# Final norm of a decoder trunk: one VectorE step folded into the squares' sum, one output piece issued from ScalarE's queue

## The chip, the cores and the metric

The kernel runs on one core of one Trainium2 chip. The metric is device time in microseconds for one launch. Three runs of the kernel before took 1069.72, 1070.24 and 1070.36 us; the median is 1070.24 us. A profile is one further execution, recorded by the hardware profiler.

## The reference

One decoder layer on 256 tokens of width 2048, in float32: a norm, a combined input projection, eight heads of forgetting attention and eight of dilated attention, an output projection with a residual add, a norm, a squared-ReLU MLP of width 8192 with a residual add, and one last norm. Cut to what matters here:

```python
def rms_norm(x, g):
    y = x * lax.rsqrt(jnp.mean(x * x, axis=-1, keepdims=True) + NORM_EPS)   # NORM_EPS = 1e-6
    return y * g

h = rms_norm(x, norm1_g);  proj = h @ w_in            # 2048 -> 6152 columns
... attention ...
x = x + mixed @ w_out
h = rms_norm(x, norm2_g)
x = x + jnp.square(jax.nn.relu(h @ w_mlp_in)) @ w_mlp_out
return rms_norm(x, final_norm_g)
```

The MLP's two products are the bulk of the work: 2048 x 8192 and 8192 x 2048 weights, 256 tokens.

## The kernel before

**Matmuls.** Every float32 matrix product is made of three products in the fast float32r format: each operand is split into a high part (`hi`, a rounded copy made by ScalarE) and a rest (`lo`, a subtraction by VectorE), and hi·hi, hi·lo and lo·hi are summed in a PSUM bank. Weights come from HBM by DMA into `raw` tiles, are split into `whi` and `wlo`, and go to TensorE. The statement `matmul(acc, a, b)` keeps `a` in the array as the stationary operand (128 columns, brought there by a weight load of its own before each matmul) and streams `b` past it as the moving operand (256 or 512 columns). A row of the profile such as `bank<-whi,mix_hi` names the moving operand first and the stationary one second. Three lines issue nearly all matmuls: L521 (products whose result is wanted transposed: the up projection of the MLP, and queries and keys; the weights are stationary, `aT_hi`/`aT_lo` move), L505 (plain products: the weights move, the activations are stationary) and L585 (a scheme that saves one in eight block products in the values' projection and in the MLP's down projection; again the weights move).

**Places in SBUF.** Tiles come from pools that are laid out one behind the other in each partition: `lead_in`, `one`, `two`, `wraw`, `wsplit`, `wide`, `few`, and behind `few` the pool `mix` during attention, which is closed before the MLP and replaced by `late5` and `late`. Tile starts are set by hand: constants such as `HIGH, LOW, NEAR` (L43) and `MIX_HI, MIX_LO` (L44), in float32 elements, are offsets inside a larger tile, and small filler tiles stand in front of others (`mix_begin` L112, `late_begin` L1238, `late_hi` and `late_low` L1246 and L1248). Weight parts go to four slots of `wsplit` and, in the MLP, to a fifth one, `whi5`/`wlo5` in `late5`: each fifth split is put there (L249). `late` holds `mix_hi` and `mix_lo`, the activations that L585 uses as stationary operands beside `big_hi` and `big_lo` of `wide`. The pool `few` holds small per-token numbers; each of its tiles takes a slot of 32 bytes per partition or a multiple of it.

**Order.** The order of the work is written out by hand: a list of half weight tiles (`steps`), each with two slots, and side work such as draining a bank that is attached to a slot (`at`). Engines run their own lists in that order.

**The end.** The last weight chunk (`last_chunk`, L1099) is done token half by token half: first 128 tokens (t = 0), then the other 128 (t = 1) as two products of 256 columns. For each, `add_down` (L1059) adds the product to the residual `xs` and, for the last columns, sums their squares on VectorE (L1070, a multiply that also accumulates, followed by a read of the accumulator into `ssq3`). `sum_before` (L1075) has summed the squares of the earlier columns into `ssq3s`, with 2048·eps added. `finish` (L1080) then makes the mean `v` (L1085), takes its power of -0.5 on GpSimd (L1086), multiplies the last columns with the gain (`put_gain`), sharpens the root by one Newton step (L1088, L1089), makes the product `ru` for ScalarE on GpSimd (L1090), and scales the row in four pieces of 384, 512, 512 and 640 columns. Pieces 0, 2 and 3 are scaled by VectorE (L1096), piece 1 by ScalarE (L1094). All four are sent to HBM from SyncE's queue (L1097), in the order 0, 1, 2, 3.

Of the kernel before, what the change touches and what calls it, by code (L numbers as in the profile page):

```python
# [11 lines left out]
F32 = mybir.dt.float32  # L12
# [3 lines left out]
ALU = mybir.AluOpType  # L16
# [3 lines left out]
P = 128  # L20
D_MODEL = 2048
# [8 lines left out]
EPS = 1e-6  # L30
# [45 lines left out]
def kernel(  # L76
# [18 lines left out]
    nc = tc.nc  # L95
    x2d = x.rearrange("b (t p) d -> p (b t) d", p=P)
    o2d = out.rearrange("b (t p) d -> p (b t) d", p=P)
# [9 lines left out]
    few = ctx.enter_context(tc.tile_pool(name="few", bufs=1))  # L107
# [893 lines left out]
    ssq3 = few.tile([P, TB, 5], F32, name="ssq3")  # L1001
    ssq3s = few.tile([P, TB], F32, name="ssq3s")
    rstd3 = few.tile([P, TB], F32, name="rstd3")
# [9 lines left out]
    def drain_d(r, c, ci):  # L1013
        for t in range(TB):
            add_down(accs[ci][t], t, slice(c * CW, (c + 1) * CW), None)
        give_back(*accs.pop(ci))
# [36 lines left out]
    def square_and_gain(t, cs, n):  # L1053
        unused = two.tile([P, CW], F32, name="nat")
        nc.scalar.activation(unused[:, :cs.stop - cs.start], xs[:, t, cs], AF.Square, accum_out=ssq3[:, t, n:n + 1])
        if n > 2:
            put_gain(t, cs)

    def add_down(acc, t, cs, n):  # L1059

        nc.vector.scalar_tensor_tensor(
            xs[:, t, cs], acc[:, :cs.stop - cs.start], rstd2sq[:, t:t + 1], xs[:, t, cs], op0=ALU.mult, op1=ALU.add
        )
        if n is not None:
            if cs.stop < D_MODEL:
                square_and_gain(t, cs, n)
            else:
                unused = two.tile([P, CW], F32, name="nat")
                unused, xc, total = unused[:, :cs.stop - cs.start], xs[:, t, cs], ssq3[:, t, n:n + 1]
                nc.vector.tensor_tensor_reduce(unused, xc, xc, 1.0, 0.0, ALU.mult, ALU.add, total)  # L1070

    def put_gain(t, cs):
        nc.vector.tensor_tensor(xs[:, t, cs], xs[:, t, cs], late_tiles["gf"][:, cs], op=ALU.mult)

    def sum_before(t, n):  # L1075
        s = ssq3s[:, t:t + 1]
        nc.vector.tensor_reduce(s, ssq3[:, t, :n], axis=mybir.AxisListType.X, op=ALU.add)
        nc.vector.tensor_scalar(s, s, D_MODEL * EPS, None, op0=ALU.add)

    def finish(t, n, cs):  # L1080
        r, s = rstd3[:, t:t + 1], ssq3s[:, t:t + 1]
        v = few.tile([P, 1], F32, name="fi_v", bufs=2)
        u = few.tile([P, 1], F32, name="fi_u", bufs=2)
        ru = few.tile([P, 1], F32, name="fi_ru", bufs=2)
        nc.vector.tensor_scalar(v, ssq3[:, t, n:n + 1], s, 1.0 / D_MODEL, op0=ALU.add, op1=ALU.mult)  # L1085
        nc.gpsimd.tensor_tensor(r, v, half_t[:, :1], op=ALU.pow)  # L1086
        put_gain(t, cs)
        nc.vector.scalar_tensor_tensor(u, r, v, r, op0=ALU.mult, op1=ALU.mult)  # L1088
        nc.vector.tensor_scalar(u, u, -0.5, 1.5, op0=ALU.mult, op1=ALU.add)  # L1089
        nc.gpsimd.tensor_tensor(ru, r, u, op=ALU.mult)  # L1090
        for c, (a, b) in enumerate(((0, 384), (384, 896), (896, 1408), (1408, 2048))):
            xc = xs[:, t, a:b]
            if c == 1:
                nc.scalar.activation(xc, xc, AF.Copy, scale=ru)  # L1094
            else:
                nc.vector.tensor_scalar(xc, xc, r, u, op0=ALU.mult, op1=ALU.mult)  # L1096
            nc.sync.dma_start(o2d[:, t, a:b], xc)  # L1097

    def last_chunk(done):  # L1099

        ci = len(chunks) - 1
        what, key, _, _, _, _, kts = chunks[ci]
        i0 = len(steps) - kts // 2
        c0 = D_MODEL - CW
        half = CW // 2
        for t, a, b, n in ((0, 0, CW, 3), (1, 0, half, 3), (1, half, CW, 4)):
            acc = take_bank()
            for kt in range(kts):
                if t == 0 and kt % 2 == 0:
                    split(done + 1 + kt // 2)  # L1110
                    load_gf()
                for c in range(a, b, half):
                    product(acc[:, c - a:c - a + half], operands(what, key), kt, t, splits[i0 + kt // 2], kt % 2,
                            slice(c, c + half), kt == 0 and c == a, kt == kts - 1, True)
                if t == 0:
                    run_side(2 * i0 + kt)
            if b == CW:
                sum_before(t, n)
            add_down(acc, t, slice(c0 + a, c0 + b), n)
            if b == CW:  # L1120
                finish(t, n, slice(c0 + a, c0 + b))
# [6 lines left out]
    for ci, (what, key, *_rest) in enumerate(chunks[:-1]):  # L1128
# [12 lines left out]
        elif what in "qk":  # L1141
# [4 lines left out]
            if what == "k":  # L1146
                kind = groups[key][4]
                for h in range(4):
                    n = e + 5 + 5 * h
# [141 lines left out]
```

## Time and profile before

| | us |
|---|---|
| median of three runs | 1070.24 |
| the profiled execution | 1070.14 |
| its span, first to last instruction | 1068.4 |
| TensorE busy | 1057.8 |
| VectorE busy | 881.1 |
| ScalarE busy | 636.5 |
| GpSimd busy | 87.6 |
| mean granted TensorE clock | 0.997 of full |

The span is what the hardware profiler saw on the core; the profiled execution's own time is 1.7 us longer, with what lies around the span. Shares of busy time overlap, since the engines work side by side. A row of the timeline gives start, duration, engine, line and operation; when rows of TensorE follow each other without a gap, the distance of their starts is what one of them costs, and not the duration in the row, since matmuls overlap. A row of the chain gives start, length and number of the instructions in one piece of the chain that ended last.

### The profile page before, as it was taken

The page shows a single profiled execution, that of the slowest core. Times are in us where ns is not written, and L with a number is a line of the kernel's source. Part 1 is how long each engine was busy: PE and PEld are TensorE (multiplying, and loading weights), DVE is VectorE, ACT ScalarE, POOL GpSimd, SP SyncE. Part 2 cuts the span into 40 slices and gives each one's busy share as a digit, 9 for nine tenths or more (in the row PEclk, how much of TensorE's full clock was granted, in tenths as well). Part 3 has the DMA queues.
Part 4 walks back from the last instruction along what each step waited for, and adds up shares of the span by engine and source line. Part 5 has one row for each costly group of instructions (what it writes and reads, how often), then busy time and mean ns, then how long its engine had stood idle before and what let it go on. Part 6 is the DMA issues. An engine that isn't in the chain of part 4 may idle for free.

```text
span 1068.4 us, 21120 instructions
## 1 busy us (share of the span) xinstructions
PE 1057.8 (99%) x8720; PEld 1031.3 (97%) x8720; DVE 881.1 (82%) x1197; ACT 636.5 (60%) x887; POOL 87.6 (8%) x90
## 2 busy tenths in 40 slices
PE   9999999999999999999999999999999999999996
PEld 8999999999988889999999999999999999999996
DVE  6687787887886666678989898988898988898996
ACT  6555556556554565566557666555666656765671
POOL 0011111101001000000100001000000010000000
PEclk9999999999999999999999999999999999999998
DMA  9765565465664567657786677766768776676752
GB/s 320 248 206 190 140 235 167 136 226 174 220 251 170 171 223 216 199 168 217 225 261 174 209 240 240 235 204 204 242 188 255 224 243 212 192 255 210 247 176 79
DMA packets 118733, 224.09 MB, mean 210 GB/s; under 512 B 4755, under 2 KB 18156, under 8 KB 118252
## 3 DMA queue, kind: packets, MB, share of 16 engines
q1 hardware_dynamic: 104684, 208.69, 57.4%
q0 software_dynamic: 13360, 13.65, 8.3%
q8 instruction: 68, 1.11, 0.4%
q10 hardware_dynamic: 592, 0.40, 0.2%
q14 instruction: 29, 0.24, 0.1%
HBM read 220.61 MB, written 2.11 MB: 208 GB/s over the span
## 4 chain that ended last, share of the span: by engine, by line
PE 99%; DMA 0%; DVE 0%; POOL 0%; ACTq 0%; DVEq 0%; issue 0%
PE bank L521 49%; PE bank L505 25%; PE bank L585 21%; PE bank L445 1%; PE bank L899 1%; PE bank L839 1%; PE bank L879 1%; DMA xs<-in_x_dram 0%; PE bank L835 0%; PE bank L901 0%; PE bank L829 0%; PE bank L833 0%; DVE xs L1096 0%; PE bank L903 0%; PE bank L663 0%; POOL rstd L1086 0%
## 5 line engine op out<-in xcount | busy, mean ns | idle before, releaser
L521 PE MATMUL bank<-aT_hi,whi 128*128 128x256 f32 x1536 | 425.0, 277 | 0.0
L521 PE MATMUL bank<-aT_hi,wlo 128*128 128x256 f32 x1536 | 424.0, 276 | 0.0
L521 PE MATMUL bank<-aT_lo,whi 128*128 128x256 f32 x1536 | 423.7, 276 | 0.0
L309 DVE TENSOR_TENSOR wlo<-raw,whi 128x1024 fp32r<-128x1024 f32 (+2 forms) x287 | 344.6, 1214 | 66.0 <-ACT whi L308 64.2
L308 ACT ACTIVATE whi<-raw 128x1024 fp32r<-128x1024 f32 (+2 forms) x288 | 296.5, 1046 | 93.8 <-PE bank L521 35.9
L521 PEld LDWEIGHTS bank<-aT_hi,whi 128*128 128x128 f32 x1536 | 288.2, 188 | 1.3 <-issue 0.6
L521 PEld LDWEIGHTS bank<-aT_lo,whi 128*128 128x128 f32 x1536 | 288.2, 188 | 0.2
L521 PEld LDWEIGHTS bank<-aT_hi,wlo 128*128 128x128 f32 x1536 | 288.1, 188 | 0.1
L271 ACT ACTIVATE whi<-raw 128x1024 fp32r<-128x1024 f32 (+1 forms) x186 | 175.0, 948 | 157.7 <-PE bank L521 68.5
L272 DVE TENSOR_TENSOR wlo<-raw,whi 128x1024 fp32r<-128x1024 f32 (+1 forms) x186 | 202.2, 1089 | 53.6 <-ACT whi L271 51.8
L505 PE MATMUL bank<-whi,big_hi 128*128 128x256 f32 (+1 forms) x456 | 141.4, 310 | 0.0
L505 PE MATMUL bank<-wlo,big_hi 128*128 128x256 f32 (+1 forms) x456 | 140.5, 308 | 0.0
L505 PE MATMUL bank<-whi,big_lo 128*128 128x256 f32 (+1 forms) x456 | 140.4, 308 | 0.0
L219 POOL DMA_DIRECT2D raw<-in_w_mlp_out_dram x42 | 50.5, 1204 | 563.7 <-DMA raw<-in_w_mlp_out_dram 340.9
L585 PE MATMUL bank<-whi,mix_hi 128*128 128x256 f32 x336 | 92.7, 276 | 0.0
L585 PE MATMUL bank<-wlo,mix_hi 128*128 128x256 f32 x336 | 92.7, 276 | 0.0
L585 PE MATMUL bank<-whi,mix_lo 128*128 128x256 f32 x336 | 92.7, 276 | 0.0
L505 PEld LDWEIGHTS bank<-wlo,big_hi 128*128 128x128 f32 x456 | 85.6, 188 | 5.2
L505 PEld LDWEIGHTS bank<-whi,big_lo 128*128 128x128 f32 x456 | 85.7, 188 | 4.5
L505 PEld LDWEIGHTS bank<-whi,big_hi 128*128 128x128 f32 x456 | 85.6, 188 | 4.5
L585 PE MATMUL bank<-whi,big_hi 128*128 128x256 f32 x252 | 69.6, 276 | 0.0
L585 PE MATMUL bank<-wlo,big_hi 128*128 128x256 f32 x252 | 69.6, 276 | 0.0
(229 smaller groups left out, 1457.5 us busy)
## 6 DMA issues: line engine op xcount, KB each, us to landing
raw<-in_w_mlp_in_dram SPq DMA_DIRECT2D x64, 1024.0 KB, 6.4
raw<-in_w_mlp_out_dram SPq DMA_DIRECT2D x64, 1024.0 KB, 6.7
raw<-in_w_in_dram SPq DMA_DIRECT2D x42, 1024.0 KB, 5.4
raw<-in_w_out_dram SPq DMA_DIRECT2D x16, 1024.0 KB, 4.9
raw<-in_w_mlp_out_dram POOLq DMA_DIRECT2D x42, 256.0 KB, 4.4
raw<-in_w_in_dram SPq DMA_DIRECT2D x4, 1040.0 KB, 10.1
xs<-in_x_dram SPq DMA_DIRECT2D x1, 2048.0 KB, 11.8
xs<-in_x_dram SPq DMA_DIRECT2D x3, 512.0 KB, 5.5
```

Of the source, the lines that this page charges most:

```text
L219: nc.gpsimd.dma_start(t[:, :2, CW // 2:CW], src[:, :2, :CW // 2], accum_op=ALU.add)
L271: nc.scalar.activation(hi, x, AF.Copy)
L272: nc.vector.tensor_tensor(lo, x, hi.bitcast(F32), op=ALU.subtract)
L308: nc.scalar.activation(hi[:, :, c:c + step], t[:, :, c:c + step], AF.Copy)
L309: nc.vector.tensor_tensor(lo, t, hi.bitcast(F32), op=ALU.subtract)
L445: nc.tensor.transpose(p[:, j * SEQ + t * P:j * SEQ + (t + 1) * P], xs[:, t, c:c + P], ident)
L505: nc.tensor.matmul(acc, x, part[:, j, cols], start=go and n == 0, stop=end and n == 2, skip_group_check=True)
L521: nc.tensor.matmul(acc, w[:, j, b * P:(b + 1) * P], a[:, kt, :], start=kt == 0 and b % 2 == 0 and n == 0, stop=kt == kts - 1 and n == 2, s ...
L585: nc.tensor.matmul(acc, a[:, k, tokens], w[:, j, n * half:(n + 1) * half], start=fresh and x == 0, stop=s == KT // 2 - 2 and j == 1 and x ...
L839: nc.tensor.matmul(s[:, c0:c1], q[:, a, h, rows], k[:, b, h, keys], start=False, stop=n == 2, skip_group_check=True)
L879: nc.tensor.transpose(p[:, j * P:(j + 1) * P], pr[:, j * P:(j + 1) * P], ident)
L899: nc.tensor.matmul(y[:, :SEQ], v[:, 0, dims], p[:, m, :SEQ], start=n == 0, stop=False, skip_group_check=True)
```

## The change

In `sum_before` the sum of the earlier squares is multiplied by 1/2048 and eps is added, so that it holds the mean of the earlier part. The last squares' sum (L1070) scales each product by 1/2048 and starts its accumulation from that number, read per token from `ssq3s`, and no longer from 0; its result in `ssq3` is then `v` itself. The instruction that made `v` is gone, and with it the tile `fi_v`. Piece 1 of the output is issued from ScalarE's queue.

```diff
-                nc.vector.tensor_tensor_reduce(unused, xc, xc, 1.0, 0.0, ALU.mult, ALU.add, total)
+                nc.vector.tensor_tensor_reduce(
+                    unused, xc, xc, 1.0 / D_MODEL, ssq3s[:, t:t + 1], ALU.mult, ALU.add, total
+                )
...
-        nc.vector.tensor_scalar(s, s, D_MODEL * EPS, None, op0=ALU.add)
+        nc.vector.tensor_scalar(s, s, 1.0 / D_MODEL, EPS, op0=ALU.mult, op1=ALU.add)
...
-        r, s = rstd3[:, t:t + 1], ssq3s[:, t:t + 1]
-        v = few.tile([P, 1], F32, name="fi_v", bufs=2)
+        r, v = rstd3[:, t:t + 1], ssq3[:, t, n:n + 1]
...
-        nc.vector.tensor_scalar(v, ssq3[:, t, n:n + 1], s, 1.0 / D_MODEL, op0=ALU.add, op1=ALU.mult)
...
-            nc.sync.dma_start(o2d[:, t, a:b], xc)
+            (nc.scalar if c == 1 else nc.sync).dma_start(o2d[:, t, a:b], xc)
```

On VectorE, the work on the last 256 columns of t = 1 stood in the kernel before as follows (`xs` is the residual row, the two `ISA` rows are the squares' sum and the read of its accumulator, `ssq_156` is `ssq3`, `raw_12357` holds the gain):

```order
L1061 SCALAR_TENSOR_TENSOR xs<-bank_12645,rstd2sq,xs 128x256
L1070 ISA nat,ssq_156<-xs 128x256
L1070 ISA ssq_156 128x1
L1085 TENSOR_SCALAR fi_v<-ssq_156,ssq3s 128x1
L1073 TENSOR_TENSOR xs<-xs,raw_12357 128x256
L1088 SCALAR_TENSOR_TENSOR fi_u<-rstd_158,fi_v 128x1
```

In the changed kernel the same place on VectorE reads:

```order
L1061 SCALAR_TENSOR_TENSOR xs<-bank_12643,rstd2sq,xs 128x256
L1070 ISA nat,ssq_156<-xs,ssq3s 128x256
L1070 ISA ssq_156 128x1
L1075 TENSOR_TENSOR xs<-xs,raw_12357 128x256
L1088 SCALAR_TENSOR_TENSOR fi_u<-rstd_158,ssq_156 128x1
```

The row of L1085 is gone, the squares' sum has `ssq3s` as one more operand, and L1088 reads `ssq3` in place of `fi_v`.

On ScalarE, the end of the program gains two rows, one for each t (the first L1055 row is the squares of earlier columns, L1094 is the scaling of piece 1):

```order
 L1055 ACTIVATE nat,ssq_156<-xs 128x512 x2
 L1094 ACTIVATE xs<-xs,fi_ru 128x512
+L1097 DMA out_dram<-xs 128x512
 L1055 ACTIVATE nat,ssq_156<-xs 128x256
 L1094 ACTIVATE xs<-xs,fi_ru 128x512
+L1097 DMA out_dram<-xs 128x512
```

Each issue stands right behind the activation whose result it sends; on SyncE's queue the 512-column piece between the 384 and the other 512 columns is gone, twice.

On TensorE no instruction is added, removed or moved. What differs there is where some operands lie. `fi_v` had two slots of 32 bytes at the end part of `few`; without it every tile of the pools behind `few` begins 64 bytes lower. Tiles of the pools ahead of it stay. In the built programs the operands of L505, L521 and L585 in the MLP begin at these bytes within a stretch of 256 (start address modulo 256):

```
operand                                   before   changed
stationary whi5 / wlo5 (L521)             96 / 224   32 / 160
stationary mix_hi / mix_lo (L585)         96 / 224   32 / 160
moving whi5, wlo5 (L505, L585)            32         224
stationary whi / wlo of wsplit (L521)     96 / 224   96 / 224
stationary big_hi / big_lo (L505, L585)   96 / 224   96 / 224
moving whi, wlo of wsplit; moving aT      32         32
```

And so many matmuls have at least one moved operand (counted in the built programs; all have 256 moving columns and belong to the MLP). The first number counts those with a high stationary part, the second those with a low one; then come the starts of moving / stationary operand, before and changed:

```
L521 aT with whi5, wlo5      368 + 184    32/96, 32/224     32/32, 32/160
L585 wsplit with mix         532 + 266    32/96, 32/224     32/32, 32/160
L585 whi5, wlo5 with mix     140 +  70    32/96, 32/224     224/32, 224/160
L505 whi5, wlo5 with big     160 +  80    32/96, 32/224     224/96, 224/224
L585 whi5, wlo5 with big     100 +  50    32/96, 32/224     224/96, 224/224
```

Attention's tiles in `mix` move too (`q`, `k`, `p`, `v_hi`, `v_lo`, from 0 to 192); 233 small matmuls have operands there. In parts of the values' projections that run before the MLP, unchanged by the edit, L585 and L505 have `aT_hi` and `aT_lo` as stationary operands, which begin at 32. In L585 the moving parts begin at 32 as well, and beside `aT` it has stationary parts kept in `xs`, which begin at 96 and 224. In the first values' projection (L505, 256 and 264 moving columns in equal number) the moving parts begin at 192, 224, 64 and 96.

## The prediction

> **What bounds the kernel now.** I read the page's busy times and its chain first, then the windows of the MLP, then the end of the span.
>
> ```profile
> span 1068.4 us, 21120 instructions
> PE 1057.8 (99%) x8720; PEld 1031.3 (97%) x8720; DVE 881.1 (82%) x1197; ACT 636.5 (60%) x887; POOL 87.6 (8%) x90
> PE 99%; DMA 0%; DVE 0%; POOL 0%; ACTq 0%; DVEq 0%; issue 0%
> ...
> 413.00:1060.00 647.00, 646.67 (x5706) 646.47 (x5705) 565.32 (x661) 399.99 (x493) 51.90 (x44) 1.00 0.69 213
> ```
>
> TensorE is the chain, 99% of it. The last row is a window over nearly all of the MLP: PE busy 646.67 of 647.00 us at granted clock 1.00, with 5706 matmuls, so 647/5706 = 113.4 ns each. VectorE has 565.32, ScalarE 399.99. Nothing keeps TensorE waiting for 647 us; whatever makes one of its matmuls longer is paid in full. The chain shows the same price in single stretches, with weights as stationary operands (L521) and with activations (L505):
>
> ```profile
> 470.11 8.16 PE bank L521 x72
> ...
> 1037.91 21.77 PE bank L505 x192
> ```
>
> 8.16/72 = 113.3 and 21.77/192 = 113.4 ns. Behind the last matmul stands the end, which is all that the edit names:
>
> ```profile
> 1059.70 0.49 DVE xs L1061
> ...
> 1060.65 0.02 DVE ssq L1070
> ...
> 1060.69 0.22 DVE fi_v L1085
> 1060.92 0.07 issue
> 1060.98 0.68 POOL rstd L1086
> ```
>
> From 1059.70 to the span's end at 1068.4 are 8.7 us, 0.8% of the time. That is the room of the two named edits.
>
> **The removed step.** L1085 begins 0.04 us after the accumulator's read (1060.65 to 1060.69), takes 0.22, and GpSimd starts 0.07 later. If L1086 follows the accumulator's read with the same 0.07, it starts at 1060.72, 0.26 earlier. The squares' sum gets an operand that is read per token, which the trace does not show for this operation. The nearest rows are two small steps of the same shape, without and with such an operand:
>
> ```profile
> 1057.03 0.15 DVE L1078 TENSOR_SCALAR ssq3s<-ssq3s 128x1 f32<-128x1 f32 x1
> 1060.69 0.21 DVE L1085 TENSOR_SCALAR fi_v<-ssq,ssq3s 128x1 f32<-128x1 f32 x1
> ```
>
> They differ by 0.06; I take that, with 0 and 0.21 (a whole step, which leaves 0.05) as bounds. Net 0.20. The number it starts from is ready at 1057.18, 3 us early, so no wait is added. `put_gain`, which stood behind L1085, runs beside the power on GpSimd (0.42 against 0.68) and stays hidden. For t = 0 the same step lies under the matmuls and counts nothing.
>
> **The second piece's issue.** The four issues of t = 1 and the transfers behind them:
>
> ```profile
> 1062.64 0.33 SPq L1097 DMA_DIRECT2D out_dram<-xs  x1
> 1063.44 0.33 SPq L1097 DMA_DIRECT2D out_dram<-xs  x1
> 1063.86 0.38 SPq L1097 DMA_DIRECT2D out_dram<-xs  x1
> 1063.86 0.87 SPq L1097 DMA_DIRECT2D out_dram<-xs  x2
> 1062.69 0.72 ACT L1094 ACTIVATE xs<-xs,fi_ru 128x512 f32<-128x512 f32 x1 [6.21 <-POOL fi_ru L1090]
> 1063.50:1064.00 0.50, 0.00 (x0) 0.00 (x0) 0.09 (x1) 0.00 (x0) 0.00 (x0) 0.50 0.95 350
> 1064.00:1064.50 0.50, 0.00 (x0) 0.00 (x0) 0.00 (x0) 0.00 (x0) 0.00 (x0) 0.50 0.51 190
> 1064.50:1065.00 0.50, 0.00 (x0) 0.00 (x0) 0.00 (x0) 0.00 (x0) 0.00 (x0) 0.50 1.03 381
> 1063.07 0.52 DVE xs L1096
> ```
>
> Piece 1 is issued at 1063.44, when ScalarE is done (1062.69 + 0.72 = 1063.41), although VectorE has piece 2 ready near 1063.07; so pieces 2 and 3 go out at 1063.86 and about 1064.3. On its own, SyncE's queue would issue piece 2 at about 1063.1. The transfers have a hole for it: the DMA engines are half busy from 1064.0 to 1064.5 (0.51), 0.25 us lost, and full right after (1.03). Once they are full the engines set the pace, so the filled hole is the most this edit can give: 0.25. Against it stands ScalarE's own issue, which at the program's start takes longer than SyncE's (quoted under the rivals). For t = 0 the issue sits on ScalarE between L1094 and the squares of L1055, which waits for L1061 until 1055.96 anyway, and the row's end is hidden by matmuls until 1059.7. I take 0.25, bounds -0.5 and +0.5. Both edits together: 0.45 us shorter.
>
> **The tile that goes.** `fi_v` took 64 bytes of `few`, so the pools behind it lie 64 bytes lower and 1950 matmuls of the MLP have an operand at another place. The trace of before has such places too, in the values' projections, where L585 takes turns between stationary parts in `aT` (start 32) and in `xs` (start 96 and 224), with moving parts at 32 in both cases:
>
> ```profile
> 211.84 0.28 PE L585 MATMUL bank<-whi,aT_hi 128*128 128x256 f32 x1
> ...
> 212.56 0.28 PE L585 MATMUL bank<-whi,xs 128*128 128x256 f32 x1
> ...
> 213.14 0.39 PE L585 MATMUL bank<-whi,xs 128*128 128x256 f32 x2
> ...
> 213.93 0.28 PE L521 MATMUL bank<-aT_hi,whi 128*128 128x256 f32 x1
> ...
> 282.40 0.28 PE L585 MATMUL bank<-whi,aT_hi 128*128 128x256 f32 x1
> ...
> 283.12 0.28 PE L585 MATMUL bank<-whi,xs 128*128 128x256 f32 x1
> ...
> 43.84 13.04 PE bank L505 x108
> ```
>
> Six matmuls with `aT` as stationary part take 0.72 us from 211.84 to 212.56 and again 0.72 from 282.40 to 283.12: 120 ns. The last seven with `xs`, from 213.14 to 213.93, take 0.79: 113 ns. Same line, same width, same moments, nothing waited for. The tile is not slow in itself: in L521 the same `aT` is the moving operand at 113.3 ns. So the start of the stationary operand matters: 96 and 224 are quick, 32 is slow. The last row is the first values' projection, stationary parts in `aT` too, moving parts at other starts (192, 224, 64, 96): 13.04/108 = 120.7 ns, where half of the matmuls have 256 and half 264 moving columns, so 113.3 x 260/256 = 115.1 were to be expected. It is 5.6 ns above.
>
> In the changed kernel 900 matmuls go from 96 to 32 with the moving part staying at 32 (532 + 368), exactly the pair seen at 120 ns; 450 from 224 to 160 (266 + 184); 210 have a stationary part at 32 or 160 and a moving one at 224 (140 + 70); and 390 keep a stationary part at 96 or 224 while the moving one goes from 32 to 224. The start 160 is not in the trace; 96 and 224, which lie 128 apart, behave alike, so I take 160 to be as 32, bounds 0 and 6.7 ns. For the 390 I take 0 by the same reasoning (only the stationary start counted where the moving one varied), bounds 0 and 6.7. The price per slow matmul: 6.7 (120.0 - 113.3) by the short runs, 5.6 by the run of 108; I take 5.6, the longer run. (900 + 450 + 210) x 5.6 = 8.7 us, all of it on the chain, because no window of the MLP has slack on PE. VectorE and ScalarE touch the moved tiles as well; VectorE has 647 - 565 = 82 us of idle time there as cover, ScalarE more. Attention's 233 small matmuls go from 0 to 192, where I know no price: 233 x 6.7 = 1.6 us either way as bound, 0 taken.
>
> **The sum.** +8.7 - 0.45 = +8.25 us on the profiled execution's own 1070.14, which lies 0.1 below the median: 1078.4 us.
>
> **The rivals.** (1) The starts don't matter, and the slow runs in the values' projections have another cause, one that the neighbours in `xs` happen to escape. Then only the end counts: 1070.14 - 0.45 = 1069.7, not slower. It decides if a weight load from 32 fits under 113 ns of streaming in the MLP as one from 96 does. For it: no stretch of the MLP itself shows a slow matmul. Against it: five of the alternations in the values' projections repeat the picture, two quoted. The Trainium skill, page "SBUF — State Buffer", section "Who interferes with whom", says that TensorE has two independent SBUF read ports, one for the moving operand and one for weight loads, and never waits on anyone; the page "TensorE: Matmul & The Clock Gate", section "LDWEIGHTS", prices a load by its columns alone, 107 ns for 128, below the 113. By these pages the shift costs nothing; the 120 ns runs disagree, and no page has the start address in a price. (2) Starts matter, but 160 counts as 224 does: (900 + 140) x 5.6 = 5.8, so 1070.14 + 5.8 - 0.45 = 1075.5. For it: the trace has no 160. (3) The moving start counts as well, so the 390 with 224 against 96 and 224 are slow too: 1950 x 5.6 = 10.9, giving 1080.6; with 6.7 ns 1082.8. For it: 224 and 96 share their distance from a multiple of 128, as 32 and 32 do in the slow pair. (4) The issue from ScalarE does not save what it should:
>
> ```profile
> 1.74 0.45 ACTq L348 DMA_DIRECT2D raw<-in_w_in_dram  x1
> ```
>
> ScalarE took 0.45 us for an issue of the same size, against 0.33 on SyncE; if its piece lands last the end is up to 0.5 longer, which moves any case by less than 1 us and decides none.
>
> **How the numbers follow.** Forecast 1078.4 (the stationary start decides, 160 as 32): 0.5. Rival 3: 0.25. Rival 2: 0.14. Rival 1: 0.11, of which nearly all lies within 0.2% (2.1 us, about what a measurement of this kernel can tell from no change). Leaving out rival 1 and the far ends, the range is 1074.0 (the 900 alone, 5.0, with the end's bound) to 1082.0. Slower by over 0.2%: 0.88; within: 0.10; faster: 0.02.
>
> **What would show it.** In the profile of the changed kernel PE stays busy without gaps through the MLP, but the chain's stretches of L585 with `mix` as stationary part come to 119 to 120 ns per matmul, every fifth half tile of L521 too, and the rest stays at 113.3. The window that held 5706 matmuls is longer by 8 to 9 us, and the time from the last matmul to the span's end is about 8.2 in place of 8.7 us. If L585 with `mix` stays at 113.3, rival 1 holds and the forecast is wrong; if only two of three of its matmuls are slow, rival 2; if L505 with every fifth half tile slows, rival 3.

## The result, and the profile after

The changed kernel took 1084.77 us (median of four runs, 1084.57 to 1084.88), the kernel before 1070.17 on the same chip (four runs, 1069.72 to 1070.36). The ratio is 1.0136, with a 95% interval of 1.0124 to 1.0147. The forecast was 1078.4 with a range to 1082: slower, as said, but by 14.6 us and not by 8.3.

The page of the changed kernel, with the lines that answer to those of before (span, busy time of each engine, shares of the chain):

```profile
span 1082.9 us, 21116 instructions
...
PE 1073.4 (99%) x8720; PEld 1046.6 (97%) x8720; DVE 881.3 (81%) x1195; ACT 637.9 (59%) x887; POOL 87.8 (8%) x90
...
PE 99%; DVE 1%; issue 0%; POOL 0%; DVEq 0%
```

TensorE's 8720 matmuls are the same and are still the whole chain, but they are busy for 1073.4 us in place of 1057.8. The other engines have hardly changed. The window of the changed kernel that holds the same part of the MLP (start and end, length, then the busy time and count of PE, PEld, DVE, ACT and POOL, granted clock, DMA share, GB/s):

```profile
413.00:1075.00 662.00, 661.49 (x5706) 661.29 (x5704) 565.85 (x660) 401.53 (x493) 52.02 (x44) 1.00 0.68 208
```

The same 5706 matmuls at the same granted clock 1.00 need 662 us and not 647: 116.0 ns each, not 113.4. No gap has opened. The chain shows in which stretches. First a piece of it before (start, length, line, number of matmuls), then the same piece in the changed kernel:

```profile
498.67 5.44 PE bank L505 x48
504.11 3.40 PE bank L585 x30
```

```profile
500.50 5.44 PE bank L505 x48
505.94 3.55 PE bank L585 x30
...
513.64 5.57 PE bank L505 x48
```

L585 went from 113.3 to 118.3 ns (3.55/30). L505 with 48 matmuls is at 113.3 in the first row and at 116.0 in the last (5.57/48), where half of its moving parts are those of the fifth slot. The timeline of the changed kernel shows the turns inside one L585 stretch; the rows between, two of each group of three, are left out:

```profile
519.04 0.28 PE L585 MATMUL bank<-whi,big_hi 128*128 128x256 f32 x1
...
519.38 0.28 PE L585 MATMUL bank<-whi,mix_hi 128*128 128x256 f32 x1
...
519.74 0.28 PE L585 MATMUL bank<-whi,big_hi 128*128 128x256 f32 x1
...
520.10 0.28 PE L585 MATMUL bank<-whi,mix_hi 128*128 128x256 f32 x1
```

Three matmuls take 0.34 us, then 0.36, then 0.36 again. The last 0.36 belongs to `big`, which has not moved; from here on, a matmul that has not moved and stands beside slow matmuls is called a neighbour. The same is seen in L521, where a half tile of the fifth slot is followed by one of `wsplit`, which has not moved either:

```profile
416.15 0.28 PE L521 MATMUL bank<-aT_hi,whi 128*128 128x256 f32 x1
...
419.02 0.29 PE L521 MATMUL bank<-aT_hi,whi 128*128 128x256 f32 x1
...
420.07 0.28 PE L521 MATMUL bank<-aT_hi,whi 128*128 128x256 f32 x1
...
421.77 0.28 PE L521 MATMUL bank<-aT_hi,whi 128*128 128x256 f32 x1
```

The 24 of the fifth slot take 119.6 ns each (2.87/24), the next nine 116.7 (1.05/9), and the fifteen after them 113.3 (1.70/15).

Summed over the program from the distances between starts of matmuls, grouped by line and by the tiles that they read (mean ns of one, before and after, and the difference of the sums):

| group | matmuls | ns | us |
|---|---|---|---|
| L585, `wsplit` with `mix` | 798 | 113.3 to 118.9 | +4.40 |
| L521, fifth slot | 552 | 113.3 to 119.3 | +3.32 |
| L585, fifth slot with `mix` | 210 | 113.3 to 117.1 | +0.79 |
| L505 and L585, fifth slot with `big` | 390 | 113.3 to 118.9 | +2.17 |
| not moved: L585, `wsplit` with `big` | 606 | 113.3 to 117.6 | +2.56 |
| not moved: L521, `wsplit` | 4056 | 114.0 to 114.3 | +1.39 |
| not moved: L505, `wsplit` with `big` | 743 | 113.3 to 113.9 | +0.42 |
| rest of the program | | | -0.23 |
| from the last product's result to the span's end | | | -0.33 |

That is 14.5 us, the difference of the two spans (1082.9 and 1068.4).

At the end, the timeline of the changed kernel reads:

```profile
1074.53 0.48 DVE L1061 SCALAR_TENSOR_TENSOR xs<-bank,rstd2sq,xs 128x256 f32<-128x256 f32 x1 [3.29 <-PE bank L505]
1075.04 0.48 DVE L1070 CUSTOM_DVE_ANT_0 nat<-xs,ssq3s 128x256 f32<-128x256 f32 x1
...
1075.57 0.42 DVE L1075 TENSOR_TENSOR xs<-xs,raw 128x256 f32<-128x256 f32 x1
...
1075.62 0.80 POOL L1086 TENSOR_TENSOR rstd<-ssq,half_t 128x1 f32<-128x1 f32 x1 [6.97 <-DVE ssq L1070]
...
1078.20 0.35 ACTq L1097 DMA_DIRECT2D out_dram<-xs  x1
```

From 1074.53 to the span's end at 1082.9 are 8.37 us, where it was 8.70. In the windows (the column before the last is the DMA share) the transfers begin in the half-busy row, at 0.51, and are full from there on; before, a half-busy row stood behind a full one:

```profile
1077.50:1078.00 0.50, 0.00 (x0) 0.00 (x0) 0.50 (x2) 0.50 (x1) 0.00 (x0) 0.71 0.00 0
1078.00:1078.50 0.50, 0.00 (x0) 0.00 (x0) 0.35 (x1) 0.17 (x1) 0.00 (x0) 0.50 0.51 187
1078.50:1079.00 0.50, 0.00 (x0) 0.00 (x0) 0.00 (x0) 0.00 (x0) 0.00 (x0) 0.50 1.02 366
1079.00:1079.50 0.50, 0.00 (x0) 0.00 (x0) 0.00 (x0) 0.00 (x0) 0.00 (x0) 0.50 1.02 389
```

### The profile page after: what moved, and what is told of

The parts are those of the page before. It is cut to its first block, busy times and chain, and to the rows that moved or that the text cites. A ratio compares the mean times of both kernels' runs of the same rounds, so it can differ in the third digit from the quotient of the medians.

```text
span 1082.9 us, 21116 instructions
## 1 busy us (share of the span) xinstructions
PE 1073.4 (99%) x8720; PEld 1046.6 (97%) x8720; DVE 881.3 (81%) x1195; ACT 637.9 (59%) x887; POOL 87.8 (8%) x90
## 4 chain that ended last, share of the span: by engine, by line
PE 99%; DVE 1%; issue 0%; POOL 0%; DVEq 0%
PE bank L521 48%; PE bank L505 25%; PE bank L585 22%; PE bank L445 1%; PE bank L839 1%; PE bank L899 1%; PE bank L391 0%; PE bank L879 0%; PE bank L835 0%; PE bank L901 0%; DVE wlo L309 0%; PE bank L829 0%; PE bank L833 0%; DVE xs L1096 0%; PE bank L903 0%
## 5 line engine op out<-in xcount | busy, mean ns | idle before, releaser
L521 PE MATMUL bank<-aT_hi,whi 128*128 128x256 f32 x1536 | 426.8, 278 | 0.0
L521 PE MATMUL bank<-aT_hi,wlo 128*128 128x256 f32 x1536 | 425.8, 278 | 0.0
L521 PE MATMUL bank<-aT_lo,whi 128*128 128x256 f32 x1536 | 425.5, 277 | 0.0
L521 PEld LDWEIGHTS bank<-aT_hi,whi 128*128 128x128 f32 x1536 | 288.5, 188 | 1.3 <-issue 0.6
L521 PEld LDWEIGHTS bank<-aT_lo,whi 128*128 128x128 f32 x1536 | 288.5, 188 | 0.2
L521 PEld LDWEIGHTS bank<-aT_hi,wlo 128*128 128x128 f32 x1536 | 288.5, 188 | 0.0
L505 PE MATMUL bank<-whi,big_hi 128*128 128x256 f32 (+1 forms) x456 | 142.0, 311 | 0.0
L505 PE MATMUL bank<-whi,big_lo 128*128 128x256 f32 (+1 forms) x456 | 141.1, 309 | 0.0
L505 PE MATMUL bank<-wlo,big_hi 128*128 128x256 f32 (+1 forms) x456 | 141.0, 309 | 0.0
L585 PE MATMUL bank<-wlo,mix_hi 128*128 128x256 f32 x336 | 94.5, 281 | 0.0
L585 PE MATMUL bank<-whi,mix_hi 128*128 128x256 f32 x336 | 94.5, 281 | 0.0
L585 PE MATMUL bank<-whi,mix_lo 128*128 128x256 f32 x336 | 94.4, 281 | 0.0
L505 PEld LDWEIGHTS bank<-wlo,big_hi 128*128 128x128 f32 x456 | 85.7, 188 | 5.1
L505 PEld LDWEIGHTS bank<-whi,big_hi 128*128 128x128 f32 x456 | 85.7, 188 | 4.5
L505 PEld LDWEIGHTS bank<-whi,big_lo 128*128 128x128 f32 x456 | 85.7, 188 | 4.5
L585 PE MATMUL bank<-whi,big_hi 128*128 128x256 f32 x252 | 70.8, 281 | 0.0
L585 PE MATMUL bank<-whi,big_lo 128*128 128x256 f32 x252 | 70.8, 281 | 0.0
```

Source lines behind the costliest of these rows:

```text
L505: nc.tensor.matmul(acc, x, part[:, j, cols], start=go and n == 0, stop=end and n == 2, skip_group_check=True)
L521: nc.tensor.matmul(acc, w[:, j, b * P:(b + 1) * P], a[:, kt, :], start=kt == 0 and b % 2 == 0 and n == 0, stop=kt == kts - 1 and n == 2, s ...
L585: nc.tensor.matmul(acc, a[:, k, tokens], w[:, j, n * half:(n + 1) * half], start=fresh and x == 0, stop=s == KT // 2 - 2 and j == 1 and x ...
```

## The experiments

**The places against the named edits.** The first two kernels separate them. In the first, the changed kernel keeps an unused tile where `fi_v` was; in the second, the kernel before gets its tiles behind `few` 64 bytes lower and nothing else.

```diff
+        few.tile([P, 1], F32, name="fi_v", bufs=2)
         r, v = rstd3[:, t:t + 1], ssq3[:, t, n:n + 1]
```

> The changed kernel with two unused slots of 32 bytes where fi_v had been, so that every tile lies as before the change; the arithmetic and the output queue stay changed. Layout theory: 1069.8 us (the end's 0.33 us of the trace below the kernel before), all matmuls of L585 and L521 in the MLP at 113.3 ns. Rival, the edits themselves (the longer squares' sum, the issue from ScalarE's queue) cost the time: 1084.8 us still.

```diff
-    mix.tile([P, 24], F32, name="mix_begin")
+    mix.tile([P, 8], F32, name="mix_begin")
...
-            late5.tile([P, 24], F32R, name="late_begin")
+            late5.tile([P, 8], F32R, name="late_begin")
```

> The kernel before with the two filler tiles ahead of mix and late5 shorter by 64 bytes, so that the pools behind few lie as in the changed kernel; no other edit. Layout theory: 1070.2 + 14.9 = 1085.1 us, a little above the changed kernel. Rival, the edits themselves: 1070.2 us.

With the tile back: 1069.73 us, ratio 0.9997 [0.9987, 1.0006]. The kernel before with its tiles lower: 1085.04 us, ratio 1.0140 [1.0123, 1.0157], although it has neither of the named edits. The window of the first and of the second:

```profile
413.00:1060.00 647.00, 646.59 (x5706) 646.39 (x5704) 565.27 (x660) 399.91 (x493) 52.03 (x44) 1.00 0.69 213
```

```profile
413.00:1075.00 662.00, 661.54 (x5706) 661.34 (x5704) 566.01 (x661) 401.58 (x493) 51.89 (x44) 1.00 0.68 208
```

So the whole loss is the 64 bytes, and the named edits have no part in it.

**The queue alone.** As the kernel with the unused tile, with all four pieces sent from SyncE.

```diff
-            (nc.scalar if c == 1 else nc.sync).dma_start(o2d[:, t, a:b], xc)
+            nc.sync.dma_start(o2d[:, t, a:b], xc)
```

> As the run before last (tiles where they were, one step less), with all four output pieces from SyncE's queue again. Time from the last matmul's result to the span's end: 8.70 us before the change, 8.37 in the changed kernel. If the removed step gives 0.20 and the queue the rest, 8.5 here and 8.37 with the queue; if the queue gives nothing, 8.4 in both; total 1069.9 us, no difference that the clock of whole runs can tell.

1070.11 us, ratio 1.0000 [0.9991, 1.0009]. In whole runs nothing can be told; in the profiles the end, from the start of L1061 on the last product to the end of the span, is 8.70 us before, 8.63 here (1059.67 to 1068.3) and 8.38 with the issue on ScalarE (1059.62 to 1068.0). In these profiles, one of each kernel, the removed step is worth 0.07 and the queue 0.25. With all four pieces from SyncE the hole in the transfers is still there (DMA share 0.61 from 1064.0 to 1064.5, between 0.88 and 1.06); with the issue on ScalarE it is gone (1.04).

**All pairs of starts.** A kernel of matmuls alone: 64 pairs of starts, 48 matmuls each with 256 moving columns.

```python
a = STEP * s + 128 * (n // 3 % 4)     # stationary: the same three times in a row
b = STEP * m + 256 * (n // 12 % 4)    # moving
```

> Not the reference's computation: nothing but 3456 float32r matmuls with 256 moving columns, 48 for each pair of start addresses (moving 0 to 224, stationary 0 to 224, in steps of 32 bytes within 256), then runs that alternate between the pairs 32/32 and 32/96, 3 and 3 of each (96 matmuls), then 12 and 36 (192 matmuls). Theory A, the stationary start alone decides: the columns 96 and 224 take 113.3 ns per matmul for every moving start, the other six 118 to 121. Theory B, the two starts have to fit each other: the quick cells lie on diagonals, such as stationary minus moving = 64 modulo 128, so 32/96 and 32/224 are quick, 32/32, 32/160, 224/96 and 224/224 slow, and 224/32, 224/160 quick. Rival, starts don't matter: all 64 cells at 113.3. Carry-over: if a slow matmul costs itself alone, the 3-and-3 run takes 96 x 116.3 = 11.2 us and the 12-and-36 run 192 x 114.8 = 22.0; if the quick ones behind it are slowed as well (as the changed kernel's trace suggests, for 6 to 9 matmuls), 11.4 and 22.2 to 22.4.

Nearly all pairs came out at 116.6 to 120 ns, moving 32 with stationary 96 among them, which the MLP runs at 113.3. Only two were quick, 96/160 and 224/32 (moving/stationary), so neither theory of the expectation holds here. In the chain of this kernel, 32/96 and then 96/160:

```profile
86.70 5.66 PE bank L57 x48
...
188.99 5.47 PE bank L63 x48
```

The test did not show what the kernel does. One thing differs: here the same weights are loaded three times in a row, while the kernel loads the high part twice and then the low one. The two mixed runs of 32/32 and 32/96 (11.40 and 22.73 us) tell nothing of neighbours, since 32/96 was slow here by itself.

**The kernel's own order.** Matmuls alone again, now in the kernel's order of three, 72 matmuls of each kind behind 48 at 119 ns. In short (`hi` and `lo` are the stationary parts, `ah` and `al` the moving ones):

```python
st = lo if n % 3 == 2 else hi          # high, high, low
mv = al if n % 3 == 1 else ah
```

> Not the reference's computation: only matmuls with 256 moving columns in the kernel's own order of three (high stationary part with the high moving part, high with low, low with high), 72 of each pattern, 48 of the changed kernel's pattern (moving 32, stationary 32 and 160) ahead of each. In the run with fixed starts nearly all pairs took 117 to 120 ns, 32/96 as well, and only 96/160 and 224/32 took 113.4, so the start of the stationary operand alone does not decide. Theory C, what counts is the order of three with low parts 128 bytes away from high ones: the kernel's own pattern 32/96, 224 at 113.3, its changed one at 119, and 32/96, 96 slow. Theory D, what counts is something of the kernel's tiles that this run does not have (their place in a larger stretch than 256): its own pattern at 118 here too. If only distances count, the patterns moved by 32, 64 and 128 as a whole behave as the unmoved one.

The chain: the place of the changed kernel (L58), the kernel before (L55), 224 with 96/224 (L61), 224 with 32/160 (L64), and 32 with 224/96, where high and low part are exchanged (L94):

```profile
25.73 5.71 PE bank L58 x48
31.44 8.18 PE bank L55 x72
...
45.34 8.53 PE bank L61 x72
...
59.58 8.18 PE bank L64 x72
...
198.94 8.56 PE bank L94 x72
```

119.0, 113.6, 118.5, 113.6 and 118.9 ns. This is the kernel's picture, and it contradicts a rule on the stationary start: 96/224 is slow behind a moving part at 224, and 32/160 is quick behind it. With all three operands 32, 64, 128 or, in one operand, 256 bytes further, the quick pair stayed quick (113.3 to 113.5 in the last 24 of each run). What these have in common is that the high stationary part begins 64 bytes behind the moving one, modulo 256. The low part need not lie 128 bytes from the high one, as theory C of the expectation had it: with both at 96 in two tiles the 72 took 113.5 ns. With one tile for all three weight loads, as in the test of all pairs, they took 117.8, so it is the repeated weights that make that test differ.

**Half of the shift.** In the changed kernel only `mix` is put back (so only the fifth slot has moved), and in another only the fifth slot is put back.

```diff
-            late.tile([P, MIX_HI], F32R, name="late_hi")
+            late.tile([P, MIX_HI + 16], F32R, name="late_hi")
```

> The changed kernel with a filler ahead of mix_hi that is 64 bytes longer: mix_hi and mix_lo begin at 96 and 224 again, only the fifth slot whi5/wlo5 stays moved (552 matmuls of L521 with stationary starts 32 and 160; 600 of L505 and L585 with moving start 224 against stationary 96 and 224). From the changed kernel's trace: 3.3 us in L521, 1.2 in L505, 1.3 to 1.7 in L585, and 0.9 to 1.5 in quick matmuls behind them: 1069.8 + 7.2 = 1077 us (1076.3 to 1078). If only the stationary start counted: 1069.8 + 3.3 = 1073.1, with matmuls behind 1073.8.

```diff
-            late5.tile([P, 24], F32R, name="late_begin")
+            late5.tile([P, 40], F32R, name="late_begin")
...
-            late.tile([P, MIX_HI], F32R, name="late_hi")
+            late.tile([P, MIX_HI - 16], F32R, name="late_hi")
```

> The changed kernel with the filler ahead of late5 64 bytes longer and the one ahead of mix_hi 64 bytes shorter: whi5 and wlo5 lie as before the change, only mix_hi and mix_lo stay moved (1008 matmuls of L585, moving 32, stationary 32 and 160; no moving start differs). If a slow matmul costs itself alone: 1008 x 5.5 = 5.5 us, 1075.3. If the quick matmuls between and behind them are slowed too (756 of L585 with big at about 118, some of L521 and L505 behind): 5.5 + 3.3 + 0.7 = 9.5 us, 1079.3.

Fifth slot moved: 1077.05 us, ratio 1.0062 [1.0047, 1.0077]. `mix` moved: 1079.47 us, ratio 1.0085 [1.0068, 1.0102]. The chain of the first: a half tile of `wsplit`, one of the fifth slot, and L585 with a `wsplit` moving part:

```profile
482.75 2.72 PE bank L521 x24
...
486.83 2.86 PE bank L521 x24
...
492.45 3.40 PE bank L585 x30
```

113.3, 119.2 and 113.3 ns: with `mix` back this L585 stretch is quick, and the fifth slot alone takes longer. The chain of the second:

```profile
485.56 2.73 PE bank L521 x24
...
491.01 3.54 PE bank L585 x30
```

Here L585 is slow (118.0) and L521 is not. In this kernel the 756 matmuls of L585 with `big` average 117.2 ns, though their operands are where they were: they take turns with `mix` in threes. That is the loss of neighbours apart from any move of their own.

**The distance.** The moving part at 32, the high stationary part 32 to 224 bytes behind it in the same order of three, and some steps finer; the low part 128 bytes from the high one, or at the same place.

```python
def apart_64(n):
    nc.tensor.matmul(**ops(n, 32, 96, 224))
```

> Not the reference's computation: only matmuls with 256 moving columns in the kernel's order of three, moving start 32 throughout, 72 of each kind, 48 with distance 0 ahead of each. The stationary start of the high part is 32 to 224 bytes behind the moving start, that of the low part 128 bytes from the high part's (first eleven kinds) or the same (last seven). Distance rule as the pattern run suggests: quick (113.3 ns once settled) only where the high part is 64 bytes behind modulo 256, whatever the low part does: kinds 64 of both series. If a period of 128 is enough: 192 of the second series is quick too. If every distance that is not a multiple of 128 were enough: nearly all kinds quick, which the first run with fixed starts speaks against. For 48, 56, 72 and 80 bytes nothing is known; a rule that goes by lines of 16 or 32 bytes would keep 72 quick or not.

The chain at distance 32, 64, 72 and at 64 with the low part at the same start:

```profile
30.96 8.51 PE bank L58 x72
...
45.18 8.19 PE bank L61 x72
...
159.10 8.48 PE bank L85 x72
...
201.87 8.17 PE bank L94 x72
```

118.2, 113.8, 117.8 and 113.5 ns over the whole runs. In the last 24 matmuls of each run the distance 64 gives 113.3 ns with either low part. Over whole runs 0, 32, 48, 56, 72, 80, 96, 128, 160, 192 and 224 give 117.8 to 121.1. Of the distances tried 64 is the only quick one, and at 64 the two places tried for the low part do equally well.

**How far a slow matmul reaches.** Slow matmuls (32 with 32/160) set among quick matmuls (32 with 96/224), and the repeated weights of the test of all pairs behind quick and behind slow matmuls.

```python
for c in (1, 2, 3, 6, 12, 24, 48):
    ...                                # 72 quick, c slow, 72 - c quick
for gap in (3, 6, 9, 12, 24):
    ...                                # six times: 3 slow, gap quick
```

> Matmuls alone, in the kernel's order of three (two with the high part, one with the low) and of 256 moving columns; nothing of the layer is computed. Quick ones have the high stationary part 64 bytes behind the moving part (32/96, 224), slow ones begin at the same place (32/32, 160). Into runs of quick ones 1, 2, 3, 6, 12, 24 and 48 slow ones are set; then groups of 3 slow ones with 3, 6, 9, 12 and 24 quick ones between them. Theory (a slow matmul holds up the quick ones behind it, as the 9 behind every fifth half tile of L521 took 117 ns): behind each slow group 6 to 9 quick matmuls take 116 to 119 ns and the next ones 113.3; with 3 or 6 quick ones between the groups nothing runs at 113.3, and with 24 between them about 15 of 24 do. Rival (each pays for itself): the first quick matmul behind a slow one is at 113.3 at once. Beside it the same weights three times in a row, at 32/96 and at 160/224, behind quick and behind slow ones: if that run only keeps the pace of what ran ahead of it, it is 113.3 behind quick ones and 118 behind slow ones; if the repeated tile itself is slow, 118 behind both.

In the timeline the quick matmuls directly behind a slow group are slow too, most of them at 117 to 121 ns: three of them in most places, five or six behind the groups of one, 12 and 24, none behind the group of two, ten behind the group of six. The changed kernel has a case of none as well: the three of `big` at 519.04 above follow slow matmuls of L505 and took 0.34 us. With 3 quick between 3 slow, all run at 117.3 to 119; with 6, the first three take 118.7 and the next three 113.3. The chain, three slow (L58) and three quick (L55), then 3 slow and 6 quick:

```profile
249.71 0.35 PE bank L58 x3
250.06 0.35 PE bank L55 x3
...
258.33 0.36 PE bank L58 x3
258.69 0.70 PE bank L55 x6
```

Three at the quick place take the same 0.35 us as three at the slow place; six take 0.70, 116 ns each. The expected six to nine neighbours were too many for a group of three, the direction is as expected, and that each matmul pays only for itself is refuted. The repeated weights, at 32/96 behind quick matmuls, at 32/96 behind slow matmuls, and at 160/224 behind quick matmuls:

```profile
25.26 10.88 PE bank L61 x96
...
41.86 11.31 PE bank L61 x96
...
58.62 11.31 PE bank L64 x96
```

The same 96 matmuls at the same place take 113.3 ns in the first case and 117.8 in the second: this order has two paces, and what ran ahead has a part in which one it takes. That fits 32/96 in the test of all pairs: 113.5 ns in the last 24 of the 96 that opened the program, 117.9 later, behind slow matmuls. It does not fit 96/160 and 224/32, which followed slow matmuls as well and were quick from the fourth matmul on; why these two of the eight pairs 64 apart were quick stays open. 160/224 is 64 apart too, and took 117.8 ns behind quick matmuls at another place, so a change of place may end the quick pace as well.

**The rule put to use.** The kernel with the unused tile; in the values' projections most moving parts of L585 go from 32 to 224 and `xs` begins 192 bytes later, so that stationary parts in `aT` and in `xs` lie 64 bytes behind them. Attention's tiles in `mix` begin 32 bytes lower as well.

```diff
-    gT = lead_in.tile([P, 56], F32, name="gT")[:, :48]
+    gT = lead_in.tile([P, 104], F32, name="gT")[:, :48]
...
+        near = LOW if chunks[ci][0] == "v" else NEAR
...
-        return one.tile([P, TB * D_MODEL + LINE - MIX_HI], kind, name="xs")
+        return one.tile([P, TB * D_MODEL + LINE - MIX_HI + 16], kind, name="xs")
...
-    mix.tile([P, 24], F32, name="mix_begin")
+    mix.tile([P, 16], F32, name="mix_begin")
```

> The changed kernel with the 64 bytes kept free and, besides, the values' projections fitted by the distance rule that the pattern run gave (stationary start of the high part minus moving start = 64 modulo 256 is quick): xs begins 192 bytes later, so that its kept parts lie at 32 and 160 as stationary operands, and the weight parts of L585 in the values' projections move from 224. 72 of 108 matmuls with aT as stationary operand and 108 of 144 with xs are then at distance 64 (before: 0 for aT, 64 for xs); the other 36 and 36, whose weight parts lie in another tile at 32, are at distance 0. Distance rule: the 72 fall from 118.6 to about 114 ns, total 0.4 to 0.5 us less than with the 64 bytes alone, 1069.2 us. If the stationary start alone decided (96 quick, 32 slow): all 252 at 118 to 119, 0.4 us more, 1070.1 us. Whole runs hardly tell these apart; the matmuls' distances in the trace do.

1069.60 us, ratio 0.9995 [0.9986, 1.0004]: no gain. By the distances of starts the 72 matmuls with `aT` that are now 64 apart went from 118.9 to 115.5 ns. But 72 others have their moving parts in a tile that stayed at 32: 36 with `aT` are still at distance 0 (118.1 to 120.6 ns), and 36 with `xs`, 24 of them with a high part that went from distance 64 to 0, rose from 116.3 to 117.7. The sum over the group is 29.05 us in place of 29.11 in the kernel before (three matmuls that waited are left out). A change of place costs something besides. Below, L586 with moving parts at 224 follows L522 with moving parts at 32 (the old L585 and L521), and the high stationary part lies 64 bytes behind the moving one in both:

```profile
134.73 0.28 PE L522 MATMUL bank<-aT_hi,wlo 128*128 128x256 f32 x1
134.85 0.28 PE L586 MATMUL bank<-whi,xs 128*128 128x256 f32 x1
...
135.21 0.28 PE L586 MATMUL bank<-whi,aT_hi 128*128 128x256 f32 x1
...
135.55 0.28 PE L586 MATMUL bank<-whi,xs 128*128 128x256 f32 x1
```

The first three behind the change take 0.36 us, the next three 0.34, which is 113 ns. So the distance is right for `aT` and `xs` alike, but it was set for only part of the matmuls. All 252 at one fitting place were not tried.

**The gain's multiplication.** In the kernel with the unused tile, `put_gain` is moved behind the scaling of piece 2.

```diff
-        put_gain(t, cs)
...
+            if c == 3:
+                put_gain(t, cs)
```

> The changed kernel with the unused tile of 64 bytes (the tiles then lie as in the kernel before), and put_gain moved from behind the squares' sum to just ahead of the fourth piece's scaling. Theory (VectorE's two-input multiplication of put_gain holds up GpSimd's power step, which took 0.80 us in the changed kernel and ended 0.42 us behind put_gain): with put_gain away the power step takes about 0.42 us, the first piece goes out about 0.35 us earlier, and from the last matrix result's eviction to the end of the span it is about 8.0 us in place of 8.38. Rival (the power step takes 0.80 us because of its new operand, whatever VectorE does): it stays at 0.80 us and the end stays at 8.4 us. In the whole run's time either is below 0.04%: 1069.4 to 1069.8 us.

1069.77 us, ratio 0.9998 [0.9989, 1.0007]. The timeline of this kernel, GpSimd's power and the L1061 from which the end counts:

```profile
1060.08 0.48 DVE L1061 SCALAR_TENSOR_TENSOR xs<-bank,rstd2sq,xs 128x256 f32<-128x256 f32 x1 [2.42 <-PE bank L505]
...
1061.17 0.55 POOL L1087 TENSOR_TENSOR rstd<-ssq,half_t 128x1 f32<-128x1 f32 x1 [6.82 <-DVE ssq L1070]
```

The power takes 0.55 in place of 0.80 (0.42 was expected), and the end is 8.12 (1060.08 to 1068.2) in place of 8.38, where 8.0 was expected. The power has the same operand as in the changed kernel, so the rival of the expectation falls: VectorE's multiplication had held GpSimd up by 0.25. The gain shows in the profile, one of each kernel, and is too small for whole runs.

## Why the prediction was wrong, step by step

**What bounds the kernel:** right. The chain stayed TensorE's, and every slow matmul was paid in full.

**The tile that goes:** the place was right, and named as the term that decides. The 1350 matmuls with a moved stationary part and a moving part that stayed were forecast at 5.6 ns each, 7.6 us; they measured 7.72 (3.32 + 4.40). Two steps failed.

First, "the start of the stationary operand matters: 96 and 224 are quick, 32 is slow". The runs show that the distance from the moving start decides. On this step hung the zero for the 390 with a moving part at 224 and stationary parts at 96 and 224: they cost 2.17 us. Rival 3 had them, at a chance of 0.25. For the 210 with 224 and stationary parts at 32 and 160 the forecast's 1.2 us was near the measured 0.79 for a wrong reason: they keep the distance of 64 and are quick by themselves, and in the kernel they stand among slow matmuls. The evidence was one-sided: of the three lines' matmuls only those with the stationary start at 32 varied the moving start, and none had 96 with another moving start than 32. "Slow at 32 whatever moves" and "slow at any distance but 64" read nearly alike there: of the four moving starts only 224 lies at 64 from 32. Its matmuls of 256 columns had a median of 118 ns all the same, in turns with others of 264; why, the runs leave open.

Second, the sum took each slow matmul to cost itself alone. Those that did not move lost 4.37 us (2.56 + 1.39 + 0.42), the largest part of the miss, and no rival had it. The trace of before had a warning beside the quoted rows, in the second alternation:

```profile
283.59 0.28 PE L585 MATMUL bank<-wlo,xs 128*128 128x256 f32 x1
...
284.50 0.28 PE L521 MATMUL bank<-aT_hi,whi 128*128 128x256 f32 x1
```

The first four with `xs`, from 283.12 to 283.59, took 117.5 ns each, and the eight up to 284.50 took 114. The prediction used the last seven of the other alternation and left out those right behind `aT`: between its own rows at 212.56 and 213.14 lie five matmuls that took 116 ns each.

**The removed step:** forecast 0.20 us, measured 0.07. The operand cost 0.06 as estimated (0.42 to 0.48). What failed is that `put_gain` "runs beside the power on GpSimd (0.42 against 0.68) and stays hidden". With the step gone `put_gain` and the power start 0.05 apart (1075.57 and 1075.62), not 0.16, and the power grew from 0.67 to 0.80. The Trainium skill, page "SBUF — State Buffer", section "Who interferes with whom", says that a VectorE instruction with two SBUF inputs contends with a GpSimd instruction that reads SBUF; the trace agrees, with 0.80 beside the multiplication and 0.55 without it.

**The second piece's issue:** forecast 0.25, measured 0.25, by the hole that was named. ScalarE's issue took 0.35.

**Rival 1** fell with the slow matmuls of the changed kernel. The page of the Trainium skill that is quoted beside it prices a load by its columns alone; at equal columns the trace has 113.3 and 118.9 ns, and the measurement decides. **Rival 2** fell because the matmuls with 160 were as slow as those with 32 (119.3 and 119.4 ns in L521). **Rival 3** was right that the moving start counts, and right about the 390. It counted the 210 as slow by themselves, which they are not, and its 1080.6 lacks the neighbours' 4.4 us.

## What to carry to other kernels

An edit that removes a small tile can move every tile behind it; compare the addresses of TensorE's operands before and after, and keep a filler where they would move. When a few rows suggest a rule on one operand, look for rows that vary the other operand too, and for what happens to the neighbours right behind; a price per instruction holds only if those keep theirs. A step taken off an engine brings its next step closer to other engines' work, so look for what then overlaps.

## What the runs showed of the hardware

With 256 moving float32r columns, a weight load before each matmul and the order high, high, low, a matmul took 113.3 ns, once settled, where the high stationary part begins 64 bytes behind the moving one (modulo 256), and 117.8 to 121.1 at the eleven other distances tried, 0 to 224. No run varied the distance at another width. It held with both operands shifted by 32, 64 or 128 bytes, and with one by 256.

Matmuls have a memory of pace: quick matmuls directly behind slow matmuls were slow too, three in most places, none in some and about ten in others. A step from one quick place to another, with the moving start going from 32 to 224, cost three slow matmuls as well. An order that loads the same weights three times ran 32/96 at 113.3 behind quick matmuls and at 117.8 behind slow matmuls; what ran ahead does not explain all of its paces.

What inside TensorE or SBUF makes 64 bytes the quick distance stays open; no run looked for it.
